# The low parts of a transformer's weights: GpSimd or VectorE outside the MLP

## The chip, the cores and the metric

The kernel runs on one core of one Trainium2 chip. The metric is the device time of one execution in microseconds (us); less is better. The kernel before was timed three times: 2446.65, 2450.95 and 2454.4 us, with a median of 2450.95 us.

## The reference

The reference is an encoder of two layers over 512 tokens of width 1024, in float32. In each layer four kinds of attention run in parallel on the same normed input, each gives 512 columns, and these are projected, gated and summed; then come attention to a memory of 256 tokens and an MLP with a squared ReLU:

```python
h = rms(x, g_mix[layer])
(aq, ak, av, bcq, bckv, bkr, cq, ck, cv, dq, dk, dv, gate) = jnp.split(h @ w_in[layer], split_points, axis=-1)
o_a = diff_attention(...); o_b = mla(...); o_c = window_gqa(...); o_d = axial_gqa(...)
o = jnp.stack([o_a, o_b, o_c, o_d], axis=2)
br = jnp.einsum('bsmc,mcd->bsmd', o, w_branch[layer])
g = jax.nn.sigmoid(gate.reshape(b, s, N_BRANCH, D_MODEL))
x = x + jnp.einsum('bsmd,bsmd->bsd', g, br) @ w_out[layer]
x = x + memory_xattn(rms(x, g_x[layer]), rms(mem, g_mem[layer]), ...)
u = rms(x, g_mlp[layer]) @ w_up[layer]
x = x + jnp.square(jax.nn.relu(u)) @ w_down[layer]
```

## The kernel before

Every product is made of three matmuls in the type float32r, for precision: each operand is split into a high part (a copy rounded to float32r) and a low part (the operand less its high part), and mm3 (L177 to L179) adds high x high, high x low and low x high. So every weight that is read from memory must be split on the chip before TensorE can use it.

That is what wload does, for one chunk of weights of 128 partitions and 640 to 1024 columns. SyncE (SP) issues the load into st, a buffer of the tag wst, of which there are two (a chain keeps these loads in the program's order). ScalarE (ACT) copies it to hi, of the tag whi with four buffers (L299; a chain keeps these copies in order too). Then lo, of the tag wlo with four buffers, is computed as st less hi by sub_lo (L167), whose last argument names the engine; without it sub_lo runs on VectorE (V). In wload of the kernel before that argument is GpSimd (G), for all 352 chunks. TensorE reads hi and lo; when it has done so, the buffers go to the next chunks. wst goes to the next load when both ACT's copy and the subtraction have read it. Other loads and stores of SP stand in the same queue: the gates' tiles in DRAM (L785), the running sum of the branches (yl, L795 to L809), the rows of relative-position bias (L255).

The key of a chunk tells what it is for: a branch's front (B, A, C, D), uqkv, gate, br (a branch's projection), out, xq, xk, xv and xo (cross-attention), up and down (the MLP). Per layer these are 4 + 16 + 8 + 8, 4, 32, 16, 8, 16, and 32 + 32.

A layer runs in this order. The mixer goes through twelve units, four of B, four of A, two of C and two of D. A unit has a front (front_B, front_A, front_G: projections in token layout, the norm of q and k, rotary embedding, the split of q and k into parts, transposes on TensorE by trans, L401) and an attention (attn_B, attn_A, attn_G: scores, softmax, transposes of the probabilities by L474, products with v). The q and k steps are small VectorE operations on a tile tok (L450 and L452 in A, L550 to L555 and L582 to L585 in C and D, L720 to L725 in B), and between them GpSimd computes the power -1/2 of the sums of squares (rpow, L309 and L310). Softmax has L496, L628, L635, L639, L758 and L761 on VectorE, and the split of the transposed probabilities L477 on ACT and L478 on VectorE. Between units the string FILL puts products that need no attention result soon: tiles of gates (gate_piece, whose result is taken from the bank df by L783) and of the branches' projections (branch_piece, L805 and L807). After the mixer come out, the cross-attention and the MLP. The MLP is the stretch from about 880 to 1250 us in the first layer and from about 2080 us to the end in the second; there VectorE and GpSimd have little besides the results of TensorE.

The order of the instructions on each engine is set by a planner at build time: it goes through the program with its own reckoning of each operation's time and issues, on each engine, what is ready, the earlier in the program first. At run time each engine works through its queue in that order, and an instruction that waits for a semaphore holds up all behind it.

Of the kernel before, what the change touches and what calls it, by code (L numbers as in the profile page):

```python
# [11 lines left out]
F32R = mybir.dt.float32r  # L12
# [4 lines left out]
P = 128  # L17
S = 512
D = 1024
# [67 lines left out]
# Products that need no attention result soon (g: a tile of gates, b: a tile of a branch's projection, k: the memory's  # L87
# keys and values), spread over the mixer: before the first unit, then one group per unit; | marks where the next
# unit's front is issued.
# [4 lines left out]
def kernel(  # L94
# [25 lines left out]
    # slots of a tag go to its tiles in program order, so early and late work use different tags  # L120
# [9 lines left out]
    def slot(dt=F32R, tag="s"):  # L130
        return tl(tag, [P, 2, S], dt)
# [52 lines left out]
    def chain(key, first, last=None):  # L184
        """issue `first` behind the chain's last instruction, on the same engine"""
        if key in tails:
            tc.add_manual_dep(first.ins, tails[key].name,
                              mybir.DependencyInfo(mybir.DependencyClass.NoSync, mybir.DependencyReason.DATA), reason=key)
        tails[key] = (last or first).ins

    def big():
        """banks of a phase of products only"""
        rot["big"] += 1
        return ("dn", "dn", "df")[(rot["big"] - 1) % 3]

    # ---------------------------------------------------------------- constants
# [11 lines left out]
    # per-layer gain tables, rebuilt at each layer's start  # L208
# [29 lines left out]
    def bias_table():  # L238
        """relative-position bias: one row per head, then sheared reads of it"""
        oh = tl("spl", [P, 1024])  # L240
        SY.dma_start(oh[:32, :1023], onehot)
        rb = tl("tok", [P, 12])
        SY.dma_start(rb[:32, :], rel)
        cm = tl("spl", [P, 1024])
        SY.dma_start(cm[:12, :1023], cmask)
        for c0, c1 in ((0, 512), (512, 1023)):
            ps = psum("dn")
            T.matmul(ps[:12, :c1 - c0], lhsT=rb[:32, :], rhs=oh[:32, c0:c1], start=True, stop=True)
            V.tensor_tensor(out=cm[:12, c0:c1], in0=ps[:12, :c1 - c0], in1=cm[:12, c0:c1], op=ALU.add)
        SY.dma_start(tscr[:, :1023], cm[:12, :1023])  # L250
# [7 lines left out]
    def layer_tables(l):  # L258
# [17 lines left out]
        # lambda: exp(sum l0*l1) - exp(sum l2*l3) + lam_init  # L276
# [14 lines left out]
    # ---------------------------------------------------------------- weights  # L291
    def wload(key, tag="wst"):
        off, n = PLAN[key]
        st = tl(tag, [P, 1024])
        i = SY.dma_start(st[:, :n], bass.AP(tensor=wts.tensor, offset=wts.offset + off, ap=[[n, P], [1, n]]))
        chain("w", i)
        hi = tl("whi", [P, 1024], F32R)
        lo = tl("wlo", [P, 1024], F32R)
        chain("wh", A.copy(hi[:, :n], st[:, :n]))  # L299
        sub_lo(lo[:, :n], st[:, :n], hi[:, :n], G)  # L300
        return hi[:, :n], lo[:, :n]
# [4 lines left out]
    # ---------------------------------------------------------------- rms of a [feature, token] operand  # L306
    def rpow(dst, src, add, n):
        """dst = (src + add) ** -0.5"""
        G.tensor_scalar(dst, src, add, None, op0=ALU.add)  # L309
        G.tensor_tensor(out=dst, in0=dst, in1=mhalf[:, :n], op=ALU.pow)  # L310

    class Norm:
        """x^T * g split into two parts; the per-token factor comes later."""
# [7 lines left out]
        def add(self, m, x, c0=0):  # L321
            """rows m of x^T, columns c0..; column parts of a row may come separately"""
# [16 lines left out]
        def add_first(self, m, x):  # L339
            """as add, spread over the engines that wait for x at the start"""  # L340
# [42 lines left out]
    # ---------------------------------------------------------------- token-layout projections  # L383
    def tok_proj(norm, views, width, evacf, half=None, tbs=range(NTB), tags=("dn",) * 4):
        """Per token block: sum over k of xg[k]^T @ W[k]."""
# [11 lines left out]
    def trans(dst, srcs, idn, rows_=P, tag="dn"):  # L397
        """PE-transpose a list of [128, n] sources into one bank, copy to dst (list-shaped view)."""
# [5 lines left out]
    def evac_sq(tk, ps, n, groups, ss, scale):  # L404
        """tk = scale * ps[:, :n]; sums of its squares per (col, heads, width, out col) group"""
# [10 lines left out]
    def split_v(hi, lo, ps, scale):  # L416
        """hi/lo parts of scale * ps; lo may be wider than hi by a broadcast"""
# [10 lines left out]
    # ---- branch A: one head (two maps) per unit  # L428
    def front_A(l, norm, h):
# [15 lines left out]
        def half(j):  # L445
# [8 lines left out]
            sk = tl("spl", [P, 2, 2, 2, 2, 64], F32R)  # m, hl, t, dup, 64  # L454
# [15 lines left out]
    def p_transpose(src, nkb, idn, dsts):  # L470
        """src [128 q, nkb*128] f32 -> bank [128 keys, nkb, 128 q] -> hi / lo destinations"""
# [58 lines left out]
    # ---- branches C and D: one key/value head and its four query heads per unit  # L530
    def front_G(l, norm, br, g):
# [14 lines left out]
        def half(j):  # L546
# [12 lines left out]
            sk = tl("spl", [P, 2, 2, 2, 64], F32R)  # t, hl, dup, 64  # L559
# [14 lines left out]
    def rope(x, tab, j, nh, nax):  # L574
        """x [P, 2 token blocks, nh, nax*32] in place: x*c + swap(x)*s, per axis of 32"""
# [11 lines left out]
    def head_pair_out(pv, of, par):  # L587
        """rows of the two halves of pv summed into of's half `par`"""
# [12 lines left out]
    def attn_G(l, u, br, g, oslots):  # L601
# [5 lines left out]
        for j in range(4):  # L607
# [39 lines left out]
            # vt holds [lo | hi | lo]: even heads read [hi | lo], odd heads [lo | hi]  # L647
# [4 lines left out]
    # ---- branch B  # L652
# [37 lines left out]
    def front_B(l, cT, p):  # L690
# [3 lines left out]
        vt = tl("v", [P, NTB, 4, 64], F32R)  # head 0: hi, lo; head 1: lo, hi  # L694
# [3 lines left out]
        for tb in range(NTB):  # L698
# [9 lines left out]
            # columns: qr0 qr1 | qn0 qn1 kn0 kn1 | v0 v1  # L708
            split_v(vt[:, tb, 0::3, :], vt[:, tb, 1:3, :], ps[:, 320:448].rearrange("p (h d) -> p h d", h=2), None)
            evac_sq(tk[:, t, :], ps, 320, [(64, 4, 64, 6 * t), (0, 2, 32, 6 * t + 4)], s, None)  # L710
        for j in range(2):
# [15 lines left out]
            sq_ = tl("spl", [P, 2, 2, 2, 96], F32R)  # hl, t, h, 96  # L727
# [44 lines left out]
    # ---------------------------------------------------------------- gates and branch projections  # L772
    def gate_piece(l, norm, bi, m):
        """tanh(gate / 2) of the bi-th branch in order, output tile m, kept in DRAM"""
# [12 lines left out]
    def branch_piece(l, bi, o, m, state):  # L787
        """y_m (+)= (1 + tanh(gate/2)) * (o @ W_b); the factor 1/2 is applied to y's sum"""
# [27 lines left out]
    # ---------------------------------------------------------------- cross-attention  # L816
    def mem_prep(l):
        """mem^T * g in two parts, and mem's per-token rms factor"""
        mg = []
        acc = tl("tok", [P, NM]) if l == 0 else None  # L820
        for c in range(2):
            st = tl("wst", [P, 4, NM])
            SY.dma_start(st, memT[c * 512:(c + 1) * 512, :].rearrange("(k p) t -> p k t", p=P))
            for k in range(4):
                if k % 2 == 0:
                    t = slot().rearrange("p a (b t) -> p a b t", b=2)  # k parity, part, tokens
# [18 lines left out]
    def mem_k(l, mg):  # L845
        KT = [tslot().rearrange("p a (b t) -> p (a b) t", b=2) for _ in range(2)]  # hi / lo: head, keys
# [12 lines left out]
    def mem_v(l):  # L859
        VX = [tslot() for _ in range(2)]  # hi / lo: key block, 4*128  # L860
# [24 lines left out]
    def xnorm_split(ps, r, gain):  # L885
        """[tok, 4 heads * 128]: per-head rms factor, optional gain, then hi/lo"""
# [13 lines left out]
    def xattn(l, norm, KT, X, nm):  # L900
# [17 lines left out]
        def attend(pr):  # L918
            for hp in range(2):
                if hp == 1 and pr == 0:  # L920
                    q_trans(1)
                pth = tl("pt", [P, 2, 2, 256], F32R)  # head, key block, q
# [63 lines left out]
    # ---------------------------------------------------------------- the trunk  # L986
# [14 lines left out]
    for l in range(L):  # L1001
# [10 lines left out]
        # mixer  # L1012
# [51 lines left out]
        # last branch, output projection and residual; the first four output tiles follow the branch's tile by tile  # L1064
# [36 lines left out]
        # cross-attention  # L1101
# [6 lines left out]
        # MLP, the hidden width in quarters  # L1108
# [46 lines left out]
def _pack(inputs):  # L1155
    """Weights regrouped into the chunks the kernel reads, each [128, n] contiguous."""
# [57 lines left out]
def _consts():  # L1214
    """Tables that depend on shapes alone."""
# [61 lines left out]
```

## Time and profile before

| | before |
|---|---|
| median of three runs | 2450.95 us |
| span of the profiled execution | 2443.1 us |
| TensorE matmuls busy | 2310.9 us |
| VectorE busy | 1564.5 us |
| ScalarE busy | 1155.5 us |
| GpSimd busy | 1059.1 us |
| granted TensorE clock, mean | 0.983 of full speed |

The profile is one execution; its span goes from the first to the last instruction, and its time with what lies around the span isn't told apart from the runs' own. A matmul's end is modelled, since matmuls are pipelined, so that a busy TensorE is not TensorE at its peak. PE is TensorE, PEld its weight loads, DVE VectorE, ACT ScalarE, POOL GpSimd, SP SyncE. L167 is line 167 of the kernel: the subtraction sub_lo of all callers, which the tiles' names tell apart (wlo for weights, spl for q and k).

### The profile page before, as it was taken

The numbers are of one execution on the slowest core, as the hardware profiler recorded it, in microseconds if no ns is written. First come the engines' busy times: TensorE is split into PE (matmuls) and PEld (weight loads), VectorE is DVE, ScalarE is ACT, GpSimd is POOL, SyncE is SP. The second block draws the span as 40 slices with busy tenths as digits, with TensorE's granted clock in tenths as the row PEclk, the third lists the DMA queues.
The fourth block names the chain that finished last, engine by engine and source line by source line (L and its number), as shares of the span: only waits on it lengthen the run. The fifth ranks groups of instructions, "written<-read, shape, count | busy, mean of one in ns | idle before, by whom it ended". The sixth has DMA issues, their size and how long they took to land.

```text
span 2443.1 us, 32530 instructions
## 1 busy us (share of the span) xinstructions
PE 2310.9 (95%) x12032; PEld 1975.2 (81%) x12032; DVE 1564.5 (64%) x2996; ACT 1155.5 (47%) x2269; POOL 1059.1 (43%) x601
## 2 busy tenths in 40 slices
PE   7999999998999999999999999999989899999999
PEld 6778988887778788888877888888877678888887
DVE  7677776788985763322557787678889758533222
ACT  4555655654653642222345565556555436422221
POOL 5443343424344455555454324353231444555553
PEclk9999999999999999999999999999989999999999
DMA  4321232352354323332332213323324442322332
GB/s 159 102 96 65 78 124 88 99 176 71 130 175 147 91 87 95 95 96 98 118 110 94 80 54 122 110 81 122 135 79 149 143 147 74 104 95 95 95 96 86
DMA packets 90944, 260.29 MB, mean 107 GB/s; under 512 B 9832, under 2 KB 14568, under 8 KB 90784
## 3 DMA queue, kind: packets, MB, share of 16 engines
q1 hardware_dynamic: 90784, 258.20, 32.2%
q8 instruction: 95, 1.56, 0.3%
q14 instruction: 65, 0.53, 0.1%
HBM read 224.56 MB, written 33.60 MB: 106 GB/s over the span
## 4 chain that ended last, share of the span: by engine, by line
PE 69%; DVE 20%; issue 4%; POOL 3%; ACT 2%; DMA 1%; SPq 0%; POOLq 0%; ACTq 0%; DVEq 0%
PE dn L177 11%; PE dn L178 11%; PE dn L179 11%; PE df L177 8%; PE df L178 8%; PE df L179 8%; DVE pt L478 2%; PE tr L474 2%; DVE p L639 1%; POOL wlo L167 1%; DVE spl L167 1%; POOL sf L310 1%; PE dn L401 1%; PE sc L177 1%; DVE sf L413 1%
## 5 line engine op out<-in xcount | busy, mean ns | idle before, releaser
L167 POOL TENSOR_TENSOR wlo<-wst,whi 128x1024 fp32r<-128x1024 f32 (+3 forms) x350 | 831.4, 2379 | 1036.2 <-ACT whi L299 933.4
L299 ACT CAST whi<-wst 128x1024 fp32r<-128x1024 f32 (+3 forms) x350 | 350.5, 1002 | 622.3 <-PE dn L178 296.6
L177 PE MATMUL df<-s,whi 128*128 128x512 f32 (+1 forms) x967 | 389.3, 403 | 22.8 <-DVE zg L783 19.4
L179 PE MATMUL df<-s,wlo 128*128 128x512 f32 (+1 forms) x967 | 381.1, 394 | 1.4 <-POOL wlo L167 1.4
L178 PE MATMUL df<-s,whi 128*128 128x512 f32 (+1 forms) x967 | 381.1, 394 | 0.3 <-DVE s L167 0.3
L177 PE MATMUL dn<-whi,s 128*128 128x384 f32 (+4 forms) x736 | 249.4, 345 | 12.3 <-ACT s L346 8.2
L178 PE MATMUL dn<-wlo,s 128*128 128x384 f32 (+4 forms) x736 | 251.1, 343 | 0.9 <-POOL wlo L167 0.9
L179 PE MATMUL dn<-whi,s 128*128 128x384 f32 (+4 forms) x736 | 249.9, 341 | 1.0 <-DVE s L347 1.0
L177 PEld LDWEIGHTS df<-s,whi 128*128 128x128 f32 x967 | 186.3, 193 | 62.7 <-DVE zg L783 20.5
L179 PEld LDWEIGHTS df<-s,wlo 128*128 128x128 f32 x967 | 185.4, 192 | 39.3 <-POOL wlo L167 2.3
L178 PEld LDWEIGHTS df<-s,whi 128*128 128x128 f32 x967 | 186.5, 193 | 35.1 <-DVE s L167 1.1
L177 PE MATMUL dn<-s,whi 128*128 128x512 f32 (+1 forms) x529 | 197.3, 376 | 2.3 <-DVE s L974 2.1
L178 PE MATMUL dn<-s,whi 128*128 128x512 f32 (+1 forms) x529 | 197.8, 375 | 0.4 <-DVE s L167 0.4
L179 PE MATMUL dn<-s,wlo 128*128 128x512 f32 (+1 forms) x529 | 197.3, 374 | 0.0
L177 PEld LDWEIGHTS dn<-whi,s 128*128 128x128 f32 x736 | 140.2, 192 | 22.5 <-ACT s L346 8.2
L478 DVE TENSOR_TENSOR pt<-tr,pt 128x512 fp32r<-128x512 f32 (+1 forms) x224 | 142.3, 642 | 19.8 <-ACT pt L477 9.8
L477 ACT CAST pt<-tr 128x512 fp32r<-128x512 f32 (+1 forms) x224 | 122.9, 556 | 59.4 <-PE tr L474 58.2
L178 PEld LDWEIGHTS dn<-wlo,s 128*128 128x128 f32 x736 | 141.0, 192 | 8.5 <-POOL wlo L167 1.3
L179 PEld LDWEIGHTS dn<-whi,s 128*128 128x128 f32 x736 | 141.0, 192 | 7.2 <-DVE s L347 1.4
L177 PEld LDWEIGHTS dn<-s,whi 128*128 128x128 f32 x529 | 99.4, 189 | 21.1 <-DVE s L974 2.5
L178 PEld LDWEIGHTS dn<-s,whi 128*128 128x128 f32 x529 | 100.1, 189 | 18.8 <-DVE s L167 0.6
L179 PEld LDWEIGHTS dn<-s,wlo 128*128 128x128 f32 x529 | 100.1, 189 | 17.7
(392 smaller groups left out, 4987.4 us busy)
## 6 DMA issues: line engine op xcount, KB each, us to landing
wst<-in_wts_dram SPq DMA_DIRECT2D x272, 512.0 KB, 3.5
wst<-in_wts_dram SPq DMA_DIRECT2D x64, 384.0 KB, 3.1
yl<-yz SPq DMA_DIRECT2D x48, 512.0 KB, 3.3
yz<-zg SPq DMA_DIRECT2D x64, 256.0 KB, 2.0
yz<-yl SPq DMA_DIRECT2D x48, 256.0 KB, 2.3
bias<-tscr SPq DMA_DIRECT2D x16, 320.0 KB, 3.2
yl<-yz SPq DMA_DIRECT2D x16, 256.0 KB, 2.6
bias<-tscr SPq DMA_DIRECT2D x8, 448.0 KB, 3.5
```

The lines of the kernel that those rows point to most:

```text
L167: (eng or V).tensor_tensor(out=dst, in0=src, in1=f(hi), op=ALU.subtract)
L177: a = T.matmul(ps, lhsT=lh, rhs=rh, start=first, stop=False)
L178: T.matmul(ps, lhsT=lh, rhs=rl, start=False, stop=False)
L179: b = T.matmul(ps, lhsT=ll, rhs=rh, start=False, stop=last)
L299: chain("wh", A.copy(hi[:, :n], st[:, :n]))
L310: G.tensor_tensor(out=dst, in0=dst, in1=mhalf[:, :n], op=ALU.pow)
L401: T.transpose(ps[:rows_, i * P:(i + 1) * P], s, idn)
L413: V.tensor_reduce(out=ss[:, o:o + nh], in_=ps[:, c0:c0 + nh * d].rearrange("p (h d) -> p h d", h=nh), axis=AX.X, op=ALU.add)
L474: T.transpose(ps[:, kb * P:(kb + 1) * P], src[:, kb * P:(kb + 1) * P], idn)
L477: A.copy(hi, pv)
L478: V.tensor_tensor(out=lo, in0=pv, in1=f(hi), op=ALU.subtract)
L639: V.tensor_scalar(e, e, st[:, 2:3], None, op0=ALU.mult)
```

## The change

The engine of one subtraction depends on the chunk's key: for up and down it stays GpSimd, for all other keys it is VectorE.

```diff
     def wload(key, tag="wst"):
...
         chain("wh", A.copy(hi[:, :n], st[:, :n]))
-        sub_lo(lo[:, :n], st[:, :n], hi[:, :n], G)
+        sub_lo(lo[:, :n], st[:, :n], hi[:, :n], G if key[1] in ("up", "down") else V)
         return hi[:, :n], lo[:, :n]
```

Besides this, comments are blanked, with the lines' numbers unchanged.

## Rows read from the trace of the kernel before

**Rows 1.** The page's first part (busy us of each engine, share of the span, instructions) and the first line of its fourth (the chain of waits that ended last, share of the span by engine); under it the same chain by line.

```profile
PE 2310.9 (95%) x12032; PEld 1975.2 (81%) x12032; DVE 1564.5 (64%) x2996; ACT 1155.5 (47%) x2269; POOL 1059.1 (43%) x601
...
PE 69%; DVE 20%; issue 4%; POOL 3%; ACT 2%; DMA 1%; SPq 0%; POOLq 0%; ACTq 0%; DVEq 0%
by line: PE dn L177 11.2%; PE dn L178 11.1%; PE dn L179 11.1%; PE df L177 8.2%; PE df L178 7.9%; PE df L179 7.8%; issue 4.2%; DVE pt L478 1.9%; PE tr L474 1.7%; DVE p L639 1.4%; POOL wlo L167 1.4%; DVE spl L167 1.2%; POOL sf L310 1.1%; PE d
```

**Rows 2.** Busy us and instructions of each engine by stretch of the span: the first mixer and cross-attention, the first MLP, the second mixer and cross-attention, and one window within the first mixer. The columns are the stretch, its length, PE, PEld, DVE, ACT, POOL, the granted clock, the DMA engines' share and GB/s.

```profile
0.00:880.00 880.00, 812.21 (x4512) 707.06 (x4513) 673.34 (x1396) 478.61 (x1013) 359.76 (x230) 0.97 0.34 113
880.00:1250.00 370.00, 370.00 (x1629) 304.92 (x1629) 135.86 (x165) 118.02 (x153) 192.04 (x87) 1.00 0.31 100
1250.00:2080.00 830.00, 771.40 (x4327) 671.07 (x4326) 635.45 (x1304) 453.29 (x966) 325.22 (x204) 0.98 0.32 108
...
610.00:671.00 61.00, 55.73 (x305) 46.12 (x304) 58.91 (x118) 38.19 (x82) 21.95 (x16) 0.97 0.40 135
```

**Rows 3.** The same by stretch for instructions that write or read the tile wlo alone: PE, PEld, POOL, clock, DMA, GB/s.

```profile
0.00:880.00 880.00, 337.10 (x922) 177.79 (x922) 265.19 (x116) 0.97 0.34 113
...
1250.00:2080.00 830.00, 317.44 (x869) 166.09 (x869) 245.53 (x109) 0.98 0.32 108
```

**Rows 4.** VectorE's instructions of six lines: shortest, median and longest duration in ns, first and last start, and the forms in them.

```profile
L807 DVE TENSOR_TENSOR yl<-yl x48: 669/691/2641, 484.4 to 1971.7; 128x512 f32<-128x512 f32 x48
L761 DVE TENSOR_SCALAR p<-p,st x64: 469/486/2610, 97.8 to 1465.8; 128x512 f32<-128x512 f32 x64
L639 DVE TENSOR_SCALAR p<-p,st x128: 398/471/2602, 457.6 to 1915.2; 128x384 f32<-128x384 f32 x64, 128x512 f32<-128x512 f32 x64
L452 DVE TENSOR_TENSOR tok<-tok,ga x32: 277/286/1903, 252.3 to 1606.2; 128x128 f32<-128x128 f32 x32
L450 DVE TENSOR_TENSOR tok<-tok,sf x16: 681/692/2443, 251.5 to 1603.7; 128x512 f32<-128x512 f32 x16
L550 DVE TENSOR_TENSOR tok<-tok,sf x16: 803/819/2979, 426.3 to 1829.0; 128x640 f32<-128x640 f32 x16
```

**Rows 5.** VectorE's groups by line and form over the whole span: count, busy us in all, mean ns of one, and the idle time of the engine just before them with what ended it.

```profile
L807 DVE TENSOR_TENSOR yl<-yl 128x512 f32<-128x512 f32 x48 | 52.8, 1101 | 0.8
L167 DVE TENSOR_TENSOR spl<-tok,spl 128x256 fp32r<-128x256 f32 x96 | 48.4, 522 | 1.3 <-ACT spl L562 0.9 <-ACT spl L729 0.2
L761 DVE TENSOR_SCALAR p<-p,st 128x512 f32<-128x512 f32 x64 | 44.5, 696 | 1.3
L639 DVE TENSOR_SCALAR p<-p,st 128x512 f32<-128x512 f32 x64 | 41.6, 654 | 0.9
L639 DVE TENSOR_SCALAR p<-p,st 128x384 f32<-128x384 f32 x64 | 36.9, 589 | 0.6
L550 DVE TENSOR_TENSOR tok<-tok,sf 128x640 f32<-128x640 f32 x16 | 23.7, 1483 | 4.5 <-POOL sf L310 4.5
L450 DVE TENSOR_TENSOR tok<-tok,sf 128x512 f32<-128x512 f32 x16 | 22.5, 1408 | 3.4 <-POOL sf L310 3.4
L452 DVE TENSOR_TENSOR tok<-tok,ga 128x128 f32<-128x128 f32 x32 | 20.9, 693 | 0.3
```

**Rows 6.** The timeline from 395 to 402 us, of GpSimd, of VectorE and of TensorE: start, duration, instruction, and in brackets the idle time before it and what ended it.

```profile
395.29 1.84 POOL L167 TENSOR_TENSOR wlo<-wst,whi 128x768 fp32r<-128x768 f32 x1
397.86 1.82 POOL L167 TENSOR_TENSOR wlo<-wst,whi 128x768 fp32r<-128x768 f32 x1
...
395.36 2.33 DVE L450 TENSOR_TENSOR tok<-tok,sf 128x512 f32<-128x512 f32 x1 [0.29 <-POOL sf L310]
397.72 2.11 DVE L452 TENSOR_TENSOR tok<-tok,ga 128x128 f32<-128x128 f32 x2
...
400.91 0.51 PE L401 MATMUL dn<-jr,spl 128*128 128x128 f32 x4 [2.63 <-DVE spl L167]
```

**Rows 7.** GpSimd's groups by line and form over the whole span, those that write wlo.

```profile
L167 POOL TENSOR_TENSOR wlo<-wst,whi 128x1024 fp32r<-128x1024 f32 x272 | 682.8, 2513 | 784.1 <-ACT whi L299 728.5 <-PE pv L768 16.4 <-ACT T L172 11.5
L167 POOL TENSOR_TENSOR wlo<-wst,whi 128x768 fp32r<-128x768 f32 x64 | 122.7, 1921 | 215.5 <-ACT whi L299 168.4 <-PE pv L646 25.2 <-PE sc L623 21.4
...
L167 POOL TENSOR_TENSOR wlo<-wst,whi 128x832 fp32r<-128x832 f32 x6 | 13.6, 2263 | 21.8 <-ACT whi L299 21.8
L167 POOL TENSOR_TENSOR wlo<-wst,whi 128x640 fp32r<-128x640 f32 x8 | 12.6, 1572 | 14.8 <-ACT whi L299 14.8
```

**Rows 8.** VectorE's groups by line and form over the whole span: two with both operands in SBUF, one in the MLP and one at the end of the cross-attention.

```profile
L1137 DVE TENSOR_TENSOR s<-s,zg 128x512 f32<-128x512 f32 x64 | 44.3, 691 | 2.2
...
L337 DVE TENSOR_TENSOR of<-of,p 128x256 f32<-128x256 f32 x28 | 11.6, 413 | 1.1 <-ACT p L336 1.1
```

**Rows 9.** Who waited for whom, over the whole span: us in all, times, the longest.

```profile
POOL wlo L167 <- ACT whi L299: 933.4, 265, 27.2
...
ACT whi L299 <- DMA wst<-in_wts_dram: 41.5, 33, 2.9
...
DVE zg L783 <- PE df L179: 37.6, 18, 4.4
...
DVE yl L805 <- PE df L179: 30.0, 20, 6.7
...
DVE yl L805 <- PE dn L179: 12.4, 3, 6.7
```

**Rows 10.** The same for SyncE's queue of DMAs.

```profile
SPq L295 <- POOL wlo L167: 1329.9, 295, 24.9
```

## The prediction

> **What bounds the kernel now.** I read the page's busy times and chain first, then the stretches by stage, then VectorE's groups by form, and last the waits.
>
> TensorE is busy for 95% of the span and has 69% of the chain of waits; VectorE has 20% of the chain (489 us of 2443.1), GpSimd 3%, and 1.4% (34 us) is the weights' subtraction on GpSimd itself [rows 1]. The reader is to see that this is an average of two kernels. In the MLP, from 880 to 1250 us and again from 2080 to the end, TensorE is busy without a break and VectorE works 37% of the time (135.9 of 370 in the first of the two). In the other 1710 us (0 to 880 and 1250 to 2080) VectorE is busy for 673.3 + 635.5 = 1309 us, 77%, and GpSimd spends 265.2 + 245.5 = 511 us on the weights' low parts [rows 2, 3]. The change touches the second part alone, so nearly all of VectorE's 489 us of chain lies there, which is 489 / 1309 = 37% of what it does there.
>
> The second thing to see is that VectorE is made slow by GpSimd. One place shows it: GpSimd starts a subtraction of 1.84 us at 395.29; VectorE's L450, which takes 0.69 us by its median, starts at 395.36 and ends when that subtraction ends, after 2.33 us; two L452 then take 2.11 us beside the next subtraction; and TensorE, whose transposes need their result, has stood for 2.63 us when they start at 400.91 [rows 4, 6]. L450's spread over the whole run is 681 to 2443 ns [rows 4]: the shortest is the operation alone, the longest is a whole subtraction on top.
>
> **The change part by part.** One call moves: the subtraction in wload, for every weight but those named up and down. Per layer there are 112 such chunks (4 + 16 + 8 + 8 of the four branches' fronts, 4 uqkv, 32 gates, 16 of the branches' projections, 8 out, 16 of the cross-attention), 224 in all; the MLP's 128 stay.
>
> *Removed from GpSimd:* the 511 us above. GpSimd keeps the small additions and powers. It isn't near its limit, so its own gain is nothing but what stood on the chain: the 34 us of [rows 1], as in the MLP GpSimd's subtractions stand beside a TensorE that doesn't pause.
>
> *Added to VectorE:* the trace has no 1024-wide subtraction on VectorE. Two undisturbed forms with both operands in SBUF give the slope: 128x512 takes 0.691 us and 128x256 takes 0.413 us [rows 8], so 0.278 us for 256 columns. That makes 0.691 + 2 x 0.278 = 1.247 us for 1024 columns, 0.969 for 768, 1.04 for 832 and 0.83 for 640. Of 1024 there are 272 less the MLP's 128, so 144; of 768 there are 64; of 832 six here and two at the start from another tile; of 640 eight [rows 7]. The sum is 144 x 1.247 + 64 x 0.969 + 8 x 1.04 + 8 x 0.83 = 257 us. Its ends: 0.691 x 2 = 1.38 us for 1024 (no fixed part, 284 us in all) and the slope alone (1.11 us, 228 us).
>
> The Trainium skill (GPSIMD Engine Reference, section 3.1) measures 2293 ns on VectorE for a float32 addition of 2048 elements, against 4497 on GpSimd; half of the first is an estimate of 1.15 us, and in proportion to the width the sum would be some 233 us. The 2.51 us that GpSimd takes here for 1024 [rows 7] is a little over half of its figure too.
>
> *Removed from VectorE:* the blocking. For a group it is the count times mean less undisturbed time [rows 4, 5]: L807 48 x (1101 - 691) = 19.7 us; L761 64 x (696 - 486) = 13.4; L639 64 x (654 - 469) + 64 x (589 - 398) = 24.1 (398 is its shortest, 469 the shortest of the same form in L761); L452 32 x (693 - 286) = 13.0; L450 16 x (1408 - 692) = 11.5; L550 16 x (1483 - 819) = 10.6. These six lines make 92 us. The same working over all of VectorE's groups outside the MLP, the many small ones with them, gives about 250 us in some 170 instructions. The lower end is the 92 us shown. The upper end is those 250, all of it gone.
>
> So VectorE's busy time changes by 257 - 250: nothing. The change exchanges time that fell on it at random for work that is in its queue.
>
> *What of it is on the path.* The blocking hits any VectorE instruction that reads SBUF, so I give it VectorE's own share: 250 x 37% = 93 us of chain. The new subtractions I price alike, 257 x 37% = 95 us. Ends: none of it (VectorE idles 1710 - 1309 = 401 us outside the MLP, more than 257), which gives 2316 in the profile, and all of it, 257 - 93 - 34 = +130, which gives 2573. I take VectorE's share, between the two: the planner puts a subtraction where VectorE is free in its own reckoning, which pulls towards none, but nothing steps over one that has begun, and an engine 77% busy leaves little room beside work that others wait for. Then 95 - 93 = +2, and what is left is GpSimd's 34 us on the chain: a net gain of 32 us.
>
> *Moved past queues.* The subtraction is the last reader of wst, so it sets when SP may issue the next weights: SP waits for it 295 times, 1330 us in all [rows 10], with gate stores, yl loads and bias reads behind it. That costs little now, because ACT's copy waits for the weights' arrival only 41.5 us in 33 times [rows 9]. On VectorE it takes half as long; if VectorE comes to it within 2.51 - 1.25 = 1.26 us the buffer is free earlier than today, if it comes later the 41.5 us grow, and I leave both at zero. On VectorE the subtraction waits for ACT's whi copy, and all of the softmax and q/k work is queued behind it; GpSimd waits there 933 us in all today [rows 9], with hardly anything behind. That is the second rival.
>
> **The rivals.**
>
> *The subtractions fill VectorE's idle time.* 401 us of idle time is enough for 257. Then the whole 93 + 34 = 127 us are won: 2443 - 127 = 2316 in the profile. For it: the blocking falls on the q/k steps that TensorE's transposes wait for, as at 400.91. Against: in the window from 610 to 671 VectorE is busy 58.9 of 61 us [rows 2], and there is no idle time for them there. Half of it, some 70 us, is as far as I believe it.
>
> *VectorE waits at the subtractions* (the slower side). VectorE's instructions that hang on the same gate and branch products are zg L783 and yl L805: they wait 37.6 + 30.0 + 12.4 = 80 us in 64 + 64 instructions, 0.63 us each [rows 9]. If each of 224 subtractions stops VectorE as long, that is 141 us, and at 37% it is 52 us of path: net -32 + 52 = +20, 2463 in the profile, 2471 as a median. It decides from 32 / (224 x 0.37) = 0.39 us of waiting per subtraction. For it: the four whi buffers are freed by TensorE, late. Against: the other low parts on VectorE wait 1.3 us in 96 instructions for ACT's copies [rows 5].
>
> Here a page speaks against the change. The Trainium skill (Perfetto Trace Analysis, section Optimizing Scalar/DVE Operations) advises moving work from a saturated VectorE to other engines, GpSimd even, but warns that these two share a read port, so that it might not help. The first half is this rival; the trace's rows at 395 us bear out the warning.
>
> *It changes nothing.* TensorE has 69% of the chain; where VectorE's delays fall beside gate and branch products that keep TensorE fed, neither the 93 nor the 95 count, and the 34 us of GpSimd shrink with them. Then the time stays within 7 us.
>
> *It doesn't remove the blocking.* GpSimd still has its powers, 174 us outside the MLP by [rows 2, 3] (359.8 + 325.2 - 510.7). If these blocked VectorE as the subtractions do, a quarter of the 250 us would be there still; but what I count as blocking was beside a subtraction in nearly all cases. That quarter is 23 of the 93 us on the path, and the net gain of 32 falls to 9, a median of 2442; I count it with no change.
>
> **How the numbers follow.** The profile's span is 2443.1 us; the median of the runs is 2450.95, 7.9 more, which I take for what lies around the span and for scatter. Forecast: 2443 - 32 = 2411, as a median 2419. A difference within 0.3% (7 us) is about what a measurement of this kernel can't tell from no change.
>
> Chances: forecast (a gain of 7 to 60 us) 0.42; idle time filled (more than 60) 0.18; no change, with the blocking kept, 0.13; VectorE waiting (slower) 0.27. So faster 0.60, same 0.13, slower 0.27. The range: below, half of the first rival and a little over, 2350; above, the second rival at 2471 and its price's upper bound (284 in place of 257 us, 10 us more at 37%), 2480. What is left out on both sides is some 2 in 10.
>
> **What the profile would show.** If the steps are right: the low-part subtraction of wlo on VectorE 224 times at 1.0 to 1.3 us and on GpSimd 128 times; L450, L452, L550 and L807 at their medians of 0.69, 0.29, 0.82 and 0.69 us; VectorE's busy time near 1570 us and GpSimd's near 550; the MLP's stretches unchanged; TensorE's waits for spl shorter. Wrong if VectorE's new subtractions stand with long idle time before them that ACT's whi ends (more than 0.4 us each), if the powers on GpSimd grow, or if TensorE waits for wlo.

## The result and the profile after

| | before | after |
|---|---|---|
| median, four runs each | 2452.41 us | 2389.94 us |
| lowest and highest | 2446.65 to 2454.40 | 2386.43 to 2391.49 |
| ratio, 95% interval | | 0.9747 (0.973 to 0.9765) |
| span of the profiled execution | 2443.1 us | 2387.4 us |
| granted TensorE clock, mean | 0.983 | 0.986 |

The change makes the kernel 62.5 us faster. The forecast was a gain of 32 us. The time lies inside the range of 2350 to 2480 us, but the gain is a little larger than the 7 to 60 us that the forecast itself stood for (chance 0.42): it falls at the lower edge of the rival that VectorE's idle time is filled (more than 60 us, 0.18).

The page of the kernel after: busy us by engine, and the chain of waits by engine; under it the chain by line.

```profile
PE 2299.4 (96%) x12032; PEld 1972.0 (83%) x12032; DVE 1547.4 (65%) x3220; ACT 1154.0 (48%) x2269; POOL 568.0 (24%) x377
...
PE 76%; DVE 14%; DMA 4%; ACT 3%; issue 2%; POOL 1%; SPq 0%; DVEq 0%; ACTq 0%; POOLq 0%
by line: PE dn L177 12.2%; PE dn L178 12.1%; PE dn L179 12.1%; PE df L177 8.8%; PE df L178 8.5%; PE df L179 8.4%; DVE wlo L167 2.5%; issue 2.1%; PE tr L474 2.0%; DMA wst<-in_wts_dram 1.6%; DVE pt L478 1.6%; PE dn L401 1.2%; PE sc L177 1.1%;
```

Beside [rows 1] the reader is to see three things. VectorE is as busy as before (1547 against 1565 us), though it runs 224 instructions more, the subtractions. GpSimd has lost half of its work (568 against 1059). And the chain has moved: VectorE from 20% to 14%, which is 489 to some 334 us, with the subtractions on VectorE (wlo, 2.5%, 60 us) among these; GpSimd from 3% to 1%.

By stretch, with the MLP now from 850 to 1220 and from 2030 us on (columns as in [rows 2]):

```profile
0.00:850.00 850.00, 801.54 (x4505) 700.23 (x4506) 663.76 (x1504) 478.17 (x1013) 115.04 (x118) 0.99 0.37 117
850.00:1220.00 370.00, 370.00 (x1629) 304.64 (x1628) 135.85 (x166) 116.63 (x151) 180.00 (x83) 1.00 0.33 100
1220.00:2030.00 810.00, 775.01 (x4366) 679.12 (x4365) 633.48 (x1428) 457.90 (x979) 93.56 (x98) 0.97 0.35 111
```

The 370 us of the first MLP hold the same 1629 matmuls as before, without a break. The two stretches outside are, by these rough cuts, 30 us (880 to 850) and 20 us (830 to 810) shorter, and VectorE's busy time in them is 663.8 + 633.5 = 1297 us against 1309.

VectorE's groups by line and form, which answer to [rows 5]:

```profile
L167 DVE TENSOR_TENSOR wlo<-wst,whi 128x1024 fp32r<-128x1024 f32 x144 | 175.1, 1218 | 31.4 <-ACT whi L299 21.9 <-PE tr L179 9.3
...
L167 DVE TENSOR_TENSOR wlo<-wst,whi 128x768 fp32r<-128x768 f32 x64 | 61.0, 953 | 10.7 <-ACT whi L299 10.6
...
L807 DVE TENSOR_TENSOR yl<-yl 128x512 f32<-128x512 f32 x48 | 33.3, 695 | 0.4
...
L639 DVE TENSOR_SCALAR p<-p,st 128x512 f32<-128x512 f32 x64 | 30.4, 484 | 0.6
L761 DVE TENSOR_SCALAR p<-p,st 128x512 f32<-128x512 f32 x64 | 30.4, 481 | 1.0
...
L639 DVE TENSOR_SCALAR p<-p,st 128x384 f32<-128x384 f32 x64 | 26.1, 413 | 0.6
...
L550 DVE TENSOR_TENSOR tok<-tok,sf 128x640 f32<-128x640 f32 x16 | 13.0, 814 | 1.7 <-POOL sf L310 1.7
...
L450 DVE TENSOR_TENSOR tok<-tok,sf 128x512 f32<-128x512 f32 x16 | 11.0, 687 | 5.5 <-POOL sf L310 5.3
...
L452 DVE TENSOR_TENSOR tok<-tok,ga 128x128 f32<-128x128 f32 x32 | 7.8, 283 | 0.1
```

Every mean has come down to within some 15 ns of the undisturbed time of before: L450 from 1408 to 687 ns, L452 from 693 to 283, L807 from 1101 to 695. The subtraction took 1.218 us for 1024 columns (1.247 was worked out). Added up over all of VectorE's groups with wlo left out, the durations fell from 1703 to 1465 us, so 238 us of blocking went, near to the 250 of the prediction.

Not every VectorE instruction that reads SBUF was blocked. L478 takes one operand from PSUM (tr) and one from SBUF (pt), and its mean is the same in both kernels (page, before and after); its longest of 224 was 695 ns before:

```profile
L478 DVE TENSOR_TENSOR pt<-tr,pt 128x512 fp32r<-128x512 f32 (+1 forms) x224 | 142.3, 642 | 19.8 <-ACT pt L477 9.8
```
```profile
L478 DVE TENSOR_TENSOR pt<-tr,pt 128x512 fp32r<-128x512 f32 (+1 forms) x224 | 143.5, 643 | 14.4 <-ACT pt L477 5.9
```

The place of [rows 6] in the kernel after, VectorE's timeline:

```profile
383.64 0.96 DVE L167 TENSOR_TENSOR wlo<-wst,whi 128x768 fp32r<-128x768 f32 x1 [0.52 <-ACT whi L299]
385.23 0.69 DVE L450 TENSOR_TENSOR tok<-tok,sf 128x512 f32<-128x512 f32 x1 [0.63 <-POOL sf L310]
...
386.87 0.48 DVE L452 TENSOR_TENSOR tok<-tok,ga 128x128 f32<-128x128 f32 x2
...
387.87 0.95 DVE L167 TENSOR_TENSOR wlo<-wst,whi 128x768 fp32r<-128x768 f32 x1
```

The same steps take 0.69 and 0.48 us in place of 2.33 and 2.11, and the subtractions stand between them in the queue, each 0.95 us.

### The profile page after: what moved, and what is told of

The parts are those of the page before. It is cut to its first block, busy times and chain, and to the rows that moved or that the text cites. A ratio compares the mean times of both kernels' runs of the same rounds, so it can differ in the third digit from the quotient of the medians.

```text
span 2387.4 us, 32501 instructions
## 1 busy us (share of the span) xinstructions
PE 2299.4 (96%) x12032; PEld 1972.0 (83%) x12032; DVE 1547.4 (65%) x3220; ACT 1154.0 (48%) x2269; POOL 568.0 (24%) x377
## 4 chain that ended last, share of the span: by engine, by line
PE 76%; DVE 14%; DMA 4%; ACT 3%; issue 2%; POOL 1%; SPq 0%; DVEq 0%; ACTq 0%; POOLq 0%
PE dn L177 12%; PE dn L178 12%; PE dn L179 12%; PE df L177 9%; PE df L178 9%; PE df L179 8%; DVE wlo L167 3%; PE tr L474 2%; DMA wst<-in_wts_dram 2%; DVE pt L478 2%; PE dn L401 1%; PE sc L177 1%; PE sc L179 1%; PE sc L178 1%; ACT whi L299 1%
## 5 line engine op out<-in xcount | busy, mean ns | idle before, releaser
L167 POOL TENSOR_TENSOR wlo<-wst,whi 128x1024 fp32r<-128x1024 f32 x128 | 327.1, 2556 | 390.9 <-ACT whi L299 390.5
L177 PE MATMUL df<-s,whi 128*128 128x512 f32 (+1 forms) x967 | 383.8, 397 | 21.4 <-DVE zg L783 7.9
L179 PE MATMUL df<-s,wlo 128*128 128x512 f32 (+1 forms) x967 | 375.8, 389 | 1.0 <-DVE wlo L167 1.0
L178 PE MATMUL df<-s,whi 128*128 128x512 f32 (+1 forms) x967 | 376.0, 389 | 0.1
L167 DVE TENSOR_TENSOR wlo<-wst,whi 128x1024 fp32r<-128x1024 f32 (+3 forms) x222 | 248.6, 1122 | 51.9 <-ACT whi L299 42.2
L177 PEld LDWEIGHTS df<-s,whi 128*128 128x128 f32 x967 | 182.6, 189 | 62.4 <-DVE zg L783 11.4
L178 PEld LDWEIGHTS df<-s,whi 128*128 128x128 f32 x967 | 182.8, 189 | 34.3 <-issue 1.1
L309 POOL TENSOR_SCALAR sf<-sf 128x8 f32<-128x8 f32 (+2 forms) x44 | 14.2, 324 | 759.3 <-DVE sf L413 713.9
L478 DVE TENSOR_TENSOR pt<-tr,pt 128x512 fp32r<-128x512 f32 (+1 forms) x224 | 143.5, 643 | 14.4 <-ACT pt L477 5.9
L177 PEld LDWEIGHTS dn<-s,whi 128*128 128x128 f32 x529 | 100.0, 190 | 23.7 <-DVE s L974 2.5
```

The source lines that it names most:

```text
L167: (eng or V).tensor_tensor(out=dst, in0=src, in1=f(hi), op=ALU.subtract)
L177: a = T.matmul(ps, lhsT=lh, rhs=rh, start=first, stop=False)
L178: T.matmul(ps, lhsT=lh, rhs=rl, start=False, stop=False)
L179: b = T.matmul(ps, lhsT=ll, rhs=rh, start=False, stop=last)
L478: V.tensor_tensor(out=lo, in0=pv, in1=f(hi), op=ALU.subtract)
```

## The experiments

Theory 1: GpSimd's subtractions, which read SBUF, stop VectorE's instructions that read SBUF, and the gain is the end of that, less what the new work costs on the path. Theory 2: the low part is ready after 1.2 in place of 2.5 us, and buffers come free earlier. Theory 3: the planner happened on a better order.

| run | median us | ratio to before (95%) |
|---|---|---|
| ghost_read | 2574.53 | 1.0498 (1.048 to 1.0515) |
| ghost_write | 2401.82 | 0.9794 (0.9776 to 0.9812) |
| no_low | 2309.99 | 0.9419 (0.9405 to 0.9434) |
| fronts_v | 2407.52 | 0.9821 (0.9806 to 0.9836) |
| fill_v | 2411.15 | 0.9835 (0.9814 to 0.9857) |
| rest_v | 2440.47 | 0.9960 (0.9944 to 0.9975) |
| double_sub | 2530.07 | 1.0327 (1.0293 to 1.0361) |
| all_v | 2385.35 | 0.9721 (0.9698 to 0.9745) |
| all_v_again | 2386.16 | 0.9748 (0.972 to 0.9775) |
| all_v_uu | 2385.86 | 0.9734 (0.9711 to 0.9757) |
| evac_23 | 2378.22 | 0.9698 (0.9683 to 0.9714) |
| evac_act | 2352.15 | 0.9598 (0.9581 to 0.9614) |

**GpSimd reads again, for nothing (ghost_read).**

```diff
+    dum = const("dum", [P, 384])
...
         sub_lo(lo[:, :n], st[:, :n], hi[:, :n], G if key[1] in ("up", "down") else V)
+        if key[1] not in ("up", "down"):
+            for c in range(0, n - 127, 384):
+                b = min(384, n - c) // 128
+                G.tensor_tensor(out=dum[:, :b * 128].rearrange("p (b c) -> p b c", b=b), in0=bc(ones, 1, b),
+                                in1=f(hi[:, c:c + b * 128]).rearrange("p (b c) -> p b c", b=b), op=ALU.subtract)
```

> The changed kernel (2390 us; the low parts outside the MLP on VectorE), with work for GpSimd added back that nobody needs: for each of the 224 chunks, two or three subtractions of up to 384 columns, whose inputs are a constant and the chunk's high part and whose output is a scratch tile. The output of the kernel stays the reference's. Theory 1 (the gain is the end of GpSimd's blocking of VectorE): the blocking comes back on top of VectorE's new work, so the 104 us of blocking that stood on the chain before return almost whole, and the time is 2470 to 2510 us, slower than before; L450's mean goes from 0.69 to over 1.1 us. Theory 2 (the gain is the low part being ready after 1.2 instead of 2.5 us, and weight buffers freed earlier): VectorE still makes the low part in 1.2 us and nothing waits for GpSimd's scratch but the high part's buffer, so the time is 2390 to 2400 us. Theory 3 (the gain is the planner's other order): no number follows, but the blocking need not come back with it.

It took 2574.5 us, 185 more than the change. VectorE's groups (L456 and L458 are L450 and L452 of the kernel after, six lines down), and GpSimd's added one, from that run:

```profile
L167 DVE TENSOR_TENSOR wlo<-wst,whi 128x1024 fp32r<-128x1024 f32 x144 | 221.6, 1540 | 17.8 <-ACT whi L300 17.3
...
L456 DVE TENSOR_TENSOR tok<-tok,sf 128x512 f32<-128x512 f32 x16 | 17.4, 1089 | 14.3 <-POOL sf L316 14.3
...
L458 DVE TENSOR_TENSOR tok<-tok,ga 128x128 f32<-128x128 f32 x32 | 13.9, 473 | 0.1
```
```profile
L305 POOL TENSOR_TENSOR dum<-ones,whi 128x384 f32<-128x384 f32 x440 | 587.8, 1336 | 517.4 <-ACT whi L300 489.7 <-ACT kr_hl L692 3.9
```

The blocking is back, and it now falls on the new subtractions too (1540 ns against 1218). The first line of the run's page:

```profile
PE 2364.1 (92%) x12032; PEld 2015.3 (78%) x12032; DVE 1768.2 (69%) x3220; ACT 1159.0 (45%) x2269; POOL 1318.9 (51%) x969
```

With as many instructions as in the change, VectorE is busy for 1768.2 in place of 1547.4 us: 221 us of stops, for 185 us of time. Theory 1 gave 2470 to 2510, too little by 65 us: the added groups were busy for 587.8 us and, in 256-wide pieces, 154.7 more, 742 us against the 511 of the kernel before. Their price, 185 / 742 = 0.25 us for each us of reading on GpSimd, is near that of the subtractions before (0.28, below). Theory 2 gave 2390 to 2400 and falls as the main cause.

**GpSimd works as much, but only writes (ghost_write).**

```diff
+    dum = const("dum", [P, 384])
...
+        if key[1] not in ("up", "down"):
+            G.tensor_copy(dum[:, 0:1], f(hi[:, 0:1]))
+            for _ in range(6):
+                G.memset(dum, 1.0)
```

> As the run with GpSimd's added subtractions, but GpSimd's added work reads SBUF only in one copy of a single column a chunk (which ties it to the high part) and then only writes: six memsets of 384 columns into the scratch tile. The output stays the reference's. If VectorE is stopped by GpSimd's reads alone, VectorE's instructions with two SBUF operands (L450, L452, L550) keep their medians of 0.69, 0.28 and 0.81 us and the time is 2390 to 2400 us; the one-operand ones (L639, L761) may still be stopped, which would be some 40 us of busy time and 10 to 15 us of time. If any work on GpSimd stops VectorE, L450's mean goes over 1.0 us and the time to 2440 or more. By theory 2 it is 2390 to 2400 us whatever the rows of L450 show.

It took 2401.8 us, 12 more than the change. The groups (five lines down here; L766 is L761):

```profile
L766 DVE TENSOR_SCALAR p<-p,st 128x512 f32<-128x512 f32 x64 | 31.6, 499 | 1.0
...
L455 DVE TENSOR_TENSOR tok<-tok,sf 128x512 f32<-128x512 f32 x16 | 11.0, 689 | 10.2 <-POOL sf L315 10.2
```
```profile
L305 POOL MEMSET dum<- 128x384 f32 x1344 | 571.2, 425 | 75.5
...
L303 POOL COPY dum<-whi 128x1 f32<-128x1 f32 x224 | 116.8, 521 | 428.6 <-ACT whi L300 421.1
```

688 us of added work on GpSimd, with the same powers queued behind it, and L450 keeps its 0.69 us; L761 goes from 481 to 499 ns, hardly more than nothing. So neither GpSimd's queue nor its being busy costs most of the time: what it reads does. Of the 12 us that are left, some may be GpSimd's queue, since ACT now waits for it to give back a whi buffer:

```profile
ACT whi L300 <- POOL dum L305: 30.7, 21, 4.3
```

The Trainium skill (SBUF — State Buffer, section Who interferes with whom) says that a VectorE instruction with two SBUF inputs contends with a GpSimd instruction that reads SBUF and not with one that only writes; L455's 689 ns here and L456's 1089 ns in the run before agree. It says too that VectorE's two-port modes contend with GpSimd; whether L766 runs in such a mode no run here shows, and its mean moves by 18 ns beside the memsets. GpSimd's added reads were all subtractions; whether its other kinds of reads stop VectorE as long wasn't tried. This pair is also what speaks against theory 3: both plans were made anew, and the time follows the blocking.

**No subtraction outside the MLP (no_low).** TensorE reads the high part in place of the low part there, so the result leaves out the low parts of the weights outside the MLP.

```diff
+        if key[1] not in ("up", "down"):
+            return hi[:, :n], hi[:, :n]
```

> The changed kernel without any subtraction outside the MLP: TensorE reads the high part in place of the low part, with the same number of matmuls, so the weights' low parts are left out of the result there. Neither GpSimd's blocking nor VectorE's added work is left, so the distance to 2390 us is the price on the path of the 222 subtractions on VectorE, and the distance to 2452 us that of the 222 on GpSimd. By the prediction's terms VectorE's cost 95 us (time 2295) and GpSimd's 127 us (2325, which doesn't fit with the first). By the chain of the changed kernel, where the wlo subtractions on VectorE are 58 us and no blocking is left, the time is 2325 to 2340 us. If the subtractions fill idle time (the first rival), it is over 2375 us.

It took 2310.0 us. So the subtractions cost 2452.4 - 2310.0 = 142 us on GpSimd and 2389.9 - 2310.0 = 80 us on VectorE. The chain (page, by engine) is TensorE's then:

```profile
PE 92%; DVE 3%; ACT 2%; DMA 2%; issue 1%; POOL 1%; SPq 0%; ACTq 0%; DVEq 0%; POOLq 0%
```

The middle expectation, 2325 to 2340 from 58 us of wlo in the chain, was too high by 15: what stands in the chain isn't all that the work costs. The busy times (page):

```profile
PE 2266.9 (98%) x12032; PEld 1960.0 (85%) x12032; DVE 1330.2 (58%) x2996; ACT 1148.4 (50%) x2269; POOL 547.6 (24%) x377
```

The same 12032 matmuls are busy for 2266.9 us here, for 2299.4 in the change and for 2310.9 in the kernel before, at granted clocks of 0.994, 0.986 and 0.983 on the mean. So some 32 of the 80 us and 44 of the 142 are matmuls that take longer, and the rest is pauses of TensorE.

**The subtractions twice on VectorE (double_sub).**

```diff
         sub_lo(lo[:, :n], st[:, :n], hi[:, :n], G if key[1] in ("up", "down") else V)
+        if key[1] not in ("up", "down"):
+            sub_lo(lo[:, :n], st[:, :n], hi[:, :n], V)
```

> The changed kernel with every subtraction outside the MLP done twice on VectorE, the second over the first (the same result). The 222 subtractions on VectorE cost 80 us of time so far (2390 against 2310 without any), a third of their 249 us of busy time. If that third is a fixed share of VectorE's work on the path, the second set costs 80 to 90 us: 2470 to 2480 us. If the first set lay in VectorE's idle time as far as there was any, the second costs more than half of its 249 us, as VectorE comes near 90% busy outside the MLP: over 2515 us. If the 80 us are mostly the waiting for ACT's high part and not the work itself, the second set, which has nothing to wait for, costs below 40 us: under 2430.

It took 2530.1 us. The first set (248.6 us of VectorE's time) cost 80 us, 32% of itself; the second, as long, costs 140 us, 56%. The second set has a higher price than the first. By stretch of the span of this run, outside the MLP (columns as in [rows 2]):

```profile
0.00:920.00 920.00, 824.07 (x4451) 710.14 (x4452) 764.75 (x1601) 475.14 (x999) 116.80 (x116) 0.96 0.34 106
1290.00:2165.00 875.00, 799.20 (x4382) 692.38 (x4383) 739.98 (x1550) 460.07 (x973) 103.96 (x101) 0.96 0.32 103
```

VectorE is busy for 1505 of 1795 us, 84%, where the change has 1297 of 1660, 78%. So it isn't full when its work costs 56%: it stops TensorE long before that.

That the price grows because idle time is used up is argued and not shown, for the second subtraction also makes the low part ready later and holds wst longer. Who waited for whom in this run:

```profile
ACT whi L299 <- DMA wst<-in_wts_dram: 112.3, 78, 4.8
PEld dn L178 <- DVE wlo L167: 13.7, 13, 4.5
```

ACT's waits for weights are 112.3 us, against 54.6 in the change. Beside ghost_read the run shows something else. Its page:

```profile
PE 2350.1 (93%) x12032; PEld 1997.8 (79%) x12032; DVE 1771.3 (70%) x3444; ACT 1161.3 (46%) x2269; POOL 588.0 (23%) x377
```

Both runs start from the change and make VectorE's busy time longer by as much, 224 us here and 221 there. (Busy time counts instructions that overlap once; the second set's own durations add up to 248.) As work in VectorE's queue that costs 140 us, as stops by GpSimd 185, of which ghost_write puts at most some 12 down to GpSimd's queue.

**The change in parts (fronts_v, fill_v, rest_v).** Each moves one group of keys to VectorE and leaves the others on GpSimd:

```diff
-        sub_lo(lo[:, :n], st[:, :n], hi[:, :n], G if key[1] in ("up", "down") else V)
+        sub_lo(lo[:, :n], st[:, :n], hi[:, :n], V if key[1] in ("A", "B", "C", "D", "uqkv") else G)  # fronts_v
+        sub_lo(lo[:, :n], st[:, :n], hi[:, :n], V if key[1] in ("gate", "br") else G)  # fill_v
+        sub_lo(lo[:, :n], st[:, :n], hi[:, :n], V if key[1] in ("out", "xq", "xk", "xv", "xo") else G)  # rest_v
```

> The change done for the fronts' weights alone (keys A, B, C, D and uqkv, 80 of the 224 chunks); gates, branches' projections, out and cross-attention stay on GpSimd. Theory 1: GpSimd's subtractions for the fronts run just when the q and k steps of VectorE do (as at 395 us), so these 80 should hold a good half of the blocking on the path: 2400 to 2425 us, against 2390 for all and 2452 for none. If the blocking counts in proportion to GpSimd's time it is 80 chunks of 224, a third, so 2430 us.

> The change done for the gates' and the branches' projections' weights alone (96 of the 224 chunks). Theory 1 with the fronts as the main place of the blocking: a gain of 10 to 25 us, 2427 to 2442 us. In proportion to GpSimd's time (96 chunks, all 1024 wide, 46% of it): 2424 us. If what counts is how early the low parts of these products are ready (theory 2), most of the gain is here, since TensorE fills its time with these products: 2400 us.

> The change done for the last third alone: out and cross-attention (48 of the 224 chunks, all of 1024 columns). The fronts alone gave 44 us and gates with branches' projections 40 us, which is 84 together, more than the 62 of the whole change. If the parts only overlap, this one gives little, 0 to 10 us (2442 to 2452); if each part is worth its share of GpSimd's time whatever the others do, it gives 48 x 2.5 of 511 us, 24%, so 15 us (2437).

Against the kernel before as timed beside them (2451.8, 2451.8 and 2449.4 us), they gain 44, 41 and 9 us. The fronts came out as theory 1 said. The gates and projections gave 41, between theory 1's figures (10 to 25, or 28 in proportion) and theory 2's 52 (2400 us), so this run alone doesn't part the two. VectorE's groups say where the blocking was: with wlo left out their durations add up to 1703 us before, 1621 in fronts_v, 1565 in fill_v and 1656 in rest_v. So 82, 138 and 47 us of blocking went (267 in sum, where the whole change took 238), the largest part with the gates and projections, and the fronts' q and k steps aren't the main place. The gains add up to 94, against 62.5 for all. Convex costs would do that: if the price on GpSimd (142) is the sum of its parts, each part costs VectorE less when it comes alone, 142 - 94 = 48 us for the three against 80 together. double_sub shows such a price; that it explains this difference is argued, not shown.

**The MLP too (all_v, all_v_again, all_v_uu).** All weights on VectorE; in all_v_uu the hidden tiles' low parts also.

```diff
-        sub_lo(lo[:, :n], st[:, :n], hi[:, :n], G if key[1] in ("up", "down") else V)
+        sub_lo(lo[:, :n], st[:, :n], hi[:, :n], V)
...
-            sub_lo(uu[:, 1, :], r, uu[:, 0, :], G if m % 2 else V)  # all_v_uu alone
+            sub_lo(uu[:, 1, :], r, uu[:, 0, :])
```

> VectorE makes the low parts of the MLP's weights too (128 more chunks, 1.22 us each, 156 us; in the MLP VectorE is busy for about 40% of the time). TensorE has no break there, so by my terms nothing is won or lost on the path: 2385 to 2395 us, and the casts L1122 of the MLP fall from 1.56 us to below 1 us in their mean, as GpSimd's subtraction beside them is gone. If VectorE in order holds up the results that TensorE's banks wait for, the MLP's stretch gets longer than its 1130 matmul-bound us of both layers and the time goes over 2400 us.

> All weights' low parts on VectorE once more, with more rounds: 2385 us, 3 to 6 us below the change as made, from the 222 + 128 subtractions none of which stands beside a GpSimd that reads at the MLP's two ends.

> All low parts of weights on VectorE, the MLP's too, and also the MLP's hidden tiles' low parts, of which every second one is on GpSimd before. GpSimd is left with powers and small sums. The MLP is bound by TensorE, so no change against the run with all weights on VectorE (2385 us): 2380 to 2390 us.

The 1130 us in the first of these is a slip of mine: the two MLPs are about 730 us. The runs took 2385.4, 2386.2 and 2385.9 us, with ratios whose intervals overlap that of the change: no difference that these runs can tell. The casts of the MLP, in the kernel after and in all_v:

```profile
L1122 DVE CAST T<-p 128x512 fp32r<-128x512 f32 x24 | 37.3, 1556 | 114.5 <-ACT p L1120 114.5
```
```profile
L1122 DVE CAST T<-p 128x512 fp32r<-128x512 f32 x24 | 10.2, 426 | 0.0
```

In the MLP each of these waits over 1.1 us for GpSimd, and the end of it gives nothing, because TensorE has no pause there. Outside the MLP the subtractions on GpSimd cost 142 us.

**Less work for VectorE (evac_act, evac_23).** Both start from all_v; the copies out of the transposes' banks, so far every second one on ScalarE, go there all (evac_act) or two of three (evac_23).

```diff
     def evac(dst, src):
         rot["ev"] += 1
-        if rot["ev"] % 2:
+        if True:  # evac_act; evac_23: if rot["ev"] % 3:
             A.copy(dst, src)
```

> All weights' low parts on VectorE, and the copies out of the banks of the q, k and p transposes (L172 and L174, taken in turn by ScalarE and VectorE so far) all on ScalarE: 80 copies of 0.68 us, 55 us, leave VectorE, which has the new work, and come to ScalarE, which is busy for half of the span. VectorE's work outside the MLP was worth 0.32 us of time for each us (the first set of subtractions) to 0.56 (the second): by that it is 55 x 0.32 to 55 x 0.56 = 18 to 31 us less, against 2386: 2355 to 2368. If ScalarE's copies come later than VectorE's did, the transposes' results are late and it is 2386 or more.

> As before it, but two of three of these copies on ScalarE in place of one of two: a third of the 80 copies on VectorE, some 18 us of them moved. A gain of 6 to 10 us against 2386 if VectorE's work is worth 0.32 to 0.56 of itself: 2376 to 2380.

2352.2 and 2378.2 us. Against all_v's 2386 these are 34 and 8 us. The first is a little over what was expected, because I had counted 80 copies and 92 moved (VectorE's instructions go from 3348 to 3256): 92 x 0.68 = 63 us, so a us of VectorE's work is worth 34 / 63 = 0.54 us of time, near the 0.56 of double_sub. In evac_23 31 copies moved, 21 us, for 0.4. Busy us of all_v and of evac_act, from their pages:

```profile
PE 2298.4 (96%) x12032; PEld 1971.9 (83%) x12032; DVE 1599.4 (67%) x3348; ACT 1153.3 (48%) x2269; POOL 242.9 (10%) x249
```
```profile
PE 2287.1 (97%) x12032; PEld 1963.5 (83%) x12032; DVE 1547.6 (66%) x3256; ACT 1194.5 (51%) x2361; POOL 233.5 (10%) x249
```

VectorE's busy time, overlaps counted once, fell by 52 us and ScalarE's grew by 41, for which it had room. evac_act is the fastest version of the study, 99 us below the kernel before.

## Why the prediction held, and which term was too small

**The bound and the blocking.** Right in the main: the MLP is untouched, the other 1660 us are bound by TensorE and VectorE in turn, and GpSimd's reads stop VectorE. All six groups fell to about their medians; VectorE's busy time was forecast near 1570 and is 1547, GpSimd's near 550 and is 568. In the runs the blocking was made to come back by GpSimd's reads (185 us) and not by its writes (12 us). Two readings were wrong. The blocking doesn't hit every VectorE instruction that reads SBUF: L478 was as fast before (642 ns) as after (643). And in [rows 6] L450 doesn't end with the subtraction beside it: that ends at 397.13 us and L450 at 397.69, so it stands for nearly the whole subtraction and does its own work after it. The place at 395 us was no measure of the gain either. TensorE's waits for spl, before and after, did get shorter, but by 5 us:

```profile
PE dn L401 <- DVE spl L167: 16.4, 12, 2.7
```
```profile
PE dn L401 <- DVE spl L167: 11.4, 11, 2.0
```

**The price of blocking on the path.** Too small: 93 us of blocking and 34 of GpSimd's own stretch on the chain make 127, and no_low measured 142. VectorE's own share of the chain, 37%, was my price. If GpSimd's 34 us are as they stand, the 250 us of blocking cost 108, 43% (45% of the 238 that went).

**The price of the new work.** Too large: 95 us by the same 37%, measured 80, 32%. (The ends of its busy time, 284 and 228 us, should read 281 and 226.) Both errors of 15 us go the same way, and together they are the 30 us between the 32 forecast and the 62.5 measured. The step that failed is to price both alike. Planned work can be put where the engine is free in the planner's reckoning, and is then partly hidden (the idea of the first rival); a stop falls on what is just running. That the first is cheaper than the second is shown by double_sub and ghost_read (140 against 185 us for as much busy time on VectorE); that the planner is why is argued. The two terms of the prediction cancelled to +2 because they had one price; its 32 us were GpSimd's 34 us alone, which no run parts from the rest of the 142.

**The rivals.** The subtractions filling the idle time was half true: 32% for the first set, 56% for the second. The gain of 62.5 us lies at the edge of what this rival stood for, with 80 us of the work on the path where it had none. VectorE waiting at the subtractions was rightly seen and over-priced. In the kernel after, who waited for whom:

```profile
DVE zg L783 <- PE df L179: 44.3, 23, 4.2
DVE wlo L167 <- ACT whi L299: 42.2, 48, 4.9
```

and the page's group of these subtractions (busy us, mean ns, idle time before):

```profile
L167 DVE TENSOR_TENSOR wlo<-wst,whi 128x1024 fp32r<-128x1024 f32 (+3 forms) x222 | 248.6, 1122 | 51.9 <-ACT whi L299 42.2
```

That is 51.9 us of idle time before 222 subtractions, 0.23 us each; the point from which it would have decided was 0.39, and the forms taken for its price (zg and yl) had 0.63. GpSimd's 933 us of waiting in [rows 9] were nearly all free time of an engine with little to do, and said nothing of VectorE. That the powers left on GpSimd would keep blocking VectorE fell too: with them there, L450's longest is 693 ns. A rest of blocking by other work is left: one L639 takes 0.86 us at 637.36, beside GpSimd's L836 (637.20 to 637.94).

**SP's queue.** Left at zero, and it wasn't quite: ACT's waits for the weights' arrival went from 41.5 [rows 9] to 54.6 us, and transfers are 4% of the chain in place of 1%:

```profile
ACT whi L299 <- DMA wst<-in_wts_dram: 54.6, 50, 3.5
```

What a third wst buffer would give wasn't tried.

## What to carry to other kernels

Read an engine's time by the spread of equal instructions: where a form's longest is its shortest plus a whole instruction of another engine, that engine may be stopping it, and the busy share shows the stop as work. A run with idle reads put back, and one with writes, shows whether it does. Moving the work to the stopped engine can then be free in its busy time and still be a gain, since here work in the queue cost less than stops of the same length: 32% against some 43% in the change, 140 against 185 us where 220 us of either were added to it. Then look for what else that engine does that one with room could take: 63 us of copies moved from VectorE to ScalarE gave 34 us more.

## What was unexpected

The stop falls on long instructions as on short ones, and hangs on what GpSimd reads: with GpSimd reading, VectorE's 1024-wide subtraction takes 1540 in place of 1218 ns, while beside 571 us of memsets VectorE's L639 and L761 take 18 to 35 ns longer in their means. And a us on VectorE has no fixed price: 0.32 for the set of subtractions that brings it to 78% busy outside the MLP, 0.56 for the set that brings it to 84% (with weights that also arrive later), 0.54 for the copies taken off it. An engine that takes turns with TensorE is a bound here long before it is full.
